# Late modulation dots issued behind the MLP's norms; other planned durations and per-head state tiles in the recurrence

## The chip, the cores and the metric

The program runs on one core of one Trainium2 chip. The metric is the device time of one execution in microseconds; the median of three runs of the kernel before is 4447.88 (4441.65 to 4450.69).

## What is computed

Two blocks follow one another. The first has two layers over a stream `x` of 512 tokens and a context `ctx` of 256, width 1024. Each layer adds a mixer and an MLP to the stream, each between norms whose gains and shifts come from the condition vector (the modulation):

```python
mod = (silu_c @ ada_w[i] + ada_b[i])[:, None, :]
mod_c = silu_cc @ ada_w[i] + ada_b[i]
sh1, sc1, gt1, sh2, sc2, gt2 = jnp.split(mod, N_MOD, axis=-1)
...
x = x + gt1 * rms_norm(y, norm_g[i, 1])
h = modulate(rms_norm(x, norm_g[i, 2]), sh2, sc2)
x = x + gt2 * rms_norm(squared_relu_mlp(h, mlp_w1[i], mlp_w2[i]), norm_g[i, 3])
```

Layer 0's mixer joins pooling and neighbourhood attention; layer 1's is a recurrence over tokens, in both directions, with 16 heads of 64:

```python
S = (S * w_t[:, :, None, :]
     - jnp.einsum('bhij,bhj->bhi', S, kk_t)[..., None] * kka_t[:, :, None, :]
     + v_t[..., None] * k_t[:, :, None, :])
y = jnp.einsum('bhij,bhj->bhi', S, inp[5]) if emit else None
```

The second block (two more layers with gated MLPs, a convolution and two attentions) takes the rest of the time, and the change doesn't touch it.

## The kernel before, in words

**Stages, by the trace's time.** Up to 85 us first sums and the memory; 85 to 440 layer 0's mixer; 440 to 560 its output product (weights `ev_o`) and the norms after it; 560 to 1060 layer 0's MLP over 76 weight blocks (`m0w`); 1060 to 1390 the shift and the products of layer 1's mixer; 1390 to 2050 the recurrence; then layer 1's MLP and the second block.

**Engines.** TensorE (PE) multiplies. Weights arrive in `wr` by a DMA on SyncE's queue (SP), 128 x 1024 in 512 KB; ScalarE (ACT) rounds them to `wh`, and VectorE (DVE), or GpSimd (POOL) for some, subtracts to get the rest `wl`. Tiles `a` hold activations, `t` temporaries, `ps`, `pj`, `ch`, `hq` PSUM results. All recorded calls stand at line 176, those of the planned list at line 171; of the two, a row is told by its tiles.

**Modulation dots.** A modulation column needs 128 x 1024 of `ada_w` (a load `ada`, 512 KB, from a ring of two buffers) and, for each of the two condition vectors (`c_rows`, `cc_rows`), one DVE instruction that multiplies, sums over the 1024 columns and writes `mod` (a dot, with its product thrown to `junk`), followed by a short read of the accumulator. `ada_dot` issues it and `ada_g` goes through the columns. The last 56 columns (8 of layer 0, 48 of layer 1; 112 dots) are issued by the generator `ada` in `second_half`. It waits for the signals of the MLP's norms, then runs woven with `chain`, `work` and others by a clock that costs each operation. That sets an order of issue; a scheduler behind it may place an instruction earlier on its engine where its data allow, and there the 112 dots stand among layer 0's mixer and its output product, ahead of 560 us.

**The recurrence.** `wkv` records all its steps in a `Plan`: 24 cells (three stages of eight pairs of heads), each with `intra` and four `step`s. `Plan.order` then builds the list of PE, ACT, DVE and POOL by simulation: an operation is ready when what it depends on has ended plus `LAT` (.2 us between engines, .06 on the same one), and of those that could start within `SLACK` of the earliest on an engine the one of lowest rank goes first. `SWITCH` is a cost on PE for a change of its tile form. The durations stand in `Step.product` and `Plan.add`. The list is then fixed (`manual_schedule`). Dependencies in the plan are by tile name.

In `step`, a product of `SC` and the state `HV` gives X; ACT copies it to `Xs`; the product `ch<-Xs,TTz` gives U for two heads, on partitions 0 to 63 and 64 to 127 of one PSUM tile; ACT copies one head's half to `HV` and DVE the other's; then the products `hq<-hv,BCt` read both. `HV` is one tile for both heads, in a ring of three:

```python
s.copy(HV[hs[0], at(st), 0], U[hs[0]])
v.tensor_copy(HV[hs[1], at(st), 1], U[hs[1]])
```

Of the kernel before, what the change touches and what calls it, by code (L numbers as in the profile page):

```python
# [2 lines left out]

# [1 line left out]

# [8 lines left out]
ALU = mybir.AluOpType  # L14
# [3 lines left out]
P = 128  # L18
# [8 lines left out]
class Clock:  # L27
# [3 lines left out]
    LAT = 0.2  # L31

    def __init__(self):
        self.free, self.wrote, self.used = {}, {}, {}
        self.now = self.end = 0.0
        self.events = {}
        self.fresh = []
        self.taken = self.given = 0
        self.plan = None

    def op(self, eng, cost, out, ins, lat=LAT):
        at = max(self.free.get(eng, 0.0), self.now)
# [111 lines left out]
class Engine:  # L154
# [5 lines left out]
    def __getattr__(self, fn):  # L160
        real, clock, eng = getattr(self._r, fn), self._c, self._n

        def call(*a, **k):
            aps = [x for x in list(a) + list(k.values()) if isinstance(x, bass.AP)]
            out = k.get("out", a[0] if a else None)
            ins = [x for x in aps if x is not out]
            outs = [out.tensor.name]
            if "accum_out" in k:
                outs.append(k["accum_out"].tensor.name)
            if clock.plan is not None:  # L170
                return clock.plan.add(eng, fn, lambda: real(*a, **k), out, ins, outs)  # L171
            if eng == "DMA":
                clock.dma(outs[0], [x.tensor.name for x in ins], out.shape[0] * _size(out) * 4)
            else:
                clock.op(eng, _cost(eng, fn, out, ins), outs, [x.tensor.name for x in ins])
            return real(*a, **k)  # L176

        setattr(self, fn, call)
        return call


class Step:
# [8 lines left out]
    def product(self, fn, out, ins):  # L191

        k, m, n = ins[0].shape[0], _size(ins[0]), _size(out)
        rows = (0, 1) if k > 64 else (int(ins[0].start_partition() >= 64),)
        cols = (0, 1) if m > 64 else (int(out.start_partition() >= 64),)
        part = [(r, x) for r in rows for x in cols]
        mode = k > 64, m > 64
        if self.mode is None:
            self.first = mode
        elif mode != self.mode:  # L200
            self.at = self.cost + 0.1
        self.mode = mode
        plain = ins[0].dtype == F32
        once = max(0.00084 * n, 0.054) if plain else 0.00042 * n + 0.003
        at = max([self.at] + [self.array.get(p, 0.0) for p in part])
        fin = at + once * (2 if plain and fn != "transpose" else 1)
        for p in part:
            self.array[p] = fin
        self.at = at + 0.006
        self.cost = max(self.cost, fin)  # L210


class Plan:
# [1 line left out]

    LAT = 0.2

    def __init__(self):  # L220
        self.steps, self.rank = [], 0
# [3 lines left out]
    def add(self, eng, fn, call, out, ins, outs):  # L225
        st = self.steps[-1] if self.steps else None
        if not (st and eng == st.eng == "PE" and st.rank[0] == self.rank):
            st = Step(eng, outs[0], (self.rank, len(self.steps)))
            self.steps.append(st)
        i = len(self.steps) - 1  # L230
        st.calls.append(call)
        for x in ins:
            t = x.tensor.name
            if t in self.writer:
                st.deps.add(self.writer[t])
            self.readers.setdefault(t, set()).add(i)
            self.touch.setdefault(t, set()).add(i)
        for t in outs:
            if t in self.writer:
                st.deps.add(self.writer[t])  # L240
            st.deps |= self.readers.get(t, set())
            self.readers[t] = set()
            self.writer[t] = i
            self.touch.setdefault(t, set()).add(i)
        st.deps.discard(i)
        if eng == "PE":
            st.product(fn, out, ins)
        elif eng == "DMA":
            st.cost = 0.1 + out.shape[0] * _size(out) * 4 / 270e3
        else:  # L250
            n = _size(out if fn != "reduce_sum" else ins[0])
            if eng == "ACT":
                st.cost = 0.17 + 0.00082 * n
            elif eng == "DVE":
                st.cost = 0.16 + 0.00105 * n
            elif fn == "tensor_tensor":
                st.cost = 0.2 + 0.0024 * n
            else:
                st.cost = 0.18 + 0.0009 * n

# [5 lines left out]
    def order(self):  # L266
        steps = self.steps
# [18 lines left out]
        mode, out = None, []  # L286
        while any(can.values()):
            best = None
            for eng, c in can.items():
                if not c:  # L290
                    continue
                f = free.get(eng, 0.0)
                at = {}
# [15 lines left out]
                i = min((x for x in at if at[x] <= lo + self.SLACK), key=lambda x: steps[x].rank)  # L309
# [20 lines left out]
                if not rest[x]:  # L330
                    room[self.place[x]].append(last[x])
            for j in s.next:
                lat = self.LAT if steps[j].eng != s.eng else 0.0 if s.eng == "PE" else 0.06
                ready[j] = max(ready[j], fin[i] + lat)
                left[j] -= 1
                if not left[j]:
                    can[steps[j].eng].add(j)
# [1 line left out]
        self.time = max(fin)  # L339
        return [steps[i] for _, i in sorted(out)]  # L340

    SWITCH = 0.1
    SLACK = 0.1


class Queues:
# [312 lines left out]
def tiles_mod(tiles):  # L659
    return [t[0] for t in tiles]  # L660
# [5 lines left out]
class First:  # L666
# [35 lines left out]
            c.nc.sync.dma_start(out[h], c.A["adaT"][i, m][:, h * 512:(h + 1) * 512])  # L702
        return out

    def ada_dot(self, i, mod, m, w, junk):

        for s in range(2):
            o = mod[s][:, m:m + 1]
            for h in range(len(w)):
                n = D // len(w)  # L710
                self.c.nc.vector.tensor_tensor_reduce(
                    out=junk[:, :n], in0=w[h], in1=self.sil[s][:, h * n:(h + 1) * n], scale=1.0,
                    scalar=o if h else self.adab[:, i, m:m + 1], op0=ALU.mult, op1=ALU.add, accum_out=o)
            yield

    def junk(self):
        return self.silp.tile([P, D], mybir.dt.bfloat16, name=self.c.nm("junk"), tag="junk")

    def ada_g(self, i, mod, ms):
        c, nc = self.c, self.c.nc  # L720
        for m in ms:
            w = c.ring(self.silp, [P, D], "ada", 2)
            nc.sync.dma_start(w, c.A["adaT"][i, m])
            yield from self.ada_dot(i, mod, m, [w], self.junk())

    def ada_tiles(self):
        c = self.c
# [468 lines left out]
    def second_half(self, yh, mtiles, mod, dr):  # L1196
# [47 lines left out]
        def ada():  # L1244

            for i in range(2):
                yield ("h", i, KD - 1)
            yield from self.ada_g(0, tiles_mod(mtiles), range(40, 48))
            self.ada_gains(0, mtiles, (3,))
            yield from self.ada1()  # L1250
            self.sil_es.close()
            odd.open()
            sig("ada1")
# [94 lines left out]
        nc.sync.dma_start(dr["mk"][l], kv)  # L1348
        yield

    def ada1(self):
        tiles = self.ada_tiles()
        self.mod1 = self.ada_out(tiles)
        yield from self.ada_g(1, tiles_mod(tiles), range(48))
        self.ada_gains(1, tiles, range(4))


# [48 lines left out]
    def cell(self, i, b, p, dr, ytm, bonus):  # L1406
# [99 lines left out]
            yield ("chain", i - 3)  # L1506


        HV = self.wt([8, 2, 64], "hv", 3)
        for h in range(2):  # L1510
            rr = np.s_[64 - h * 64:128 - h * 64]
            for d in range(2):
                nc.sync.dma_start(HV[rr, d * 4:(d + 1) * 4, h], dr["v"][tok[d], p * P + h * 64:p * P + (h + 1) * 64].rearrange("(c s) f -> s c f", s=64))
        for h in range(2):
            rr = np.s_[h * 64:(h + 1) * 64]
            g.tensor_copy(HV[rr, 0:8:7, h], self.H[p][rr])
        SC, BCt, TT = yield from self.intra(i, out, BC, AQ)
        done("intra")
        for st in range(4):
# [115 lines left out]
    def step(self, p, qd, st, SC, BCt, TT, Qz, HV, wc, ytm):  # L1635
# [10 lines left out]
        half = lambda: c.bank("ch", (P, 2, 64))  # L1646
        X = half()
        for d, h in DH:
            mm(X[hs[h], d], SC[d][:, h, chs[d], :64], HV[:, es[d], h], start=d == 0, stop=d == 1)
        Xs = self.wt([2, 64], "Xs", 3)  # L1650
        s.copy(Xs, X)
        HQ = c.bank("hq", (P, 2, 2, 64))
        HU, Q = HQ[:, 0], HQ[:, 1]
        for d, h in DH:
            mm(HU[hs[h], d], c.ident[:, hs[h]], HV[:, es[d], h], start=d == 0, stop=False)
        if out:

            for h, d in DH:
                mm(Q[hs[d], h], Qz[:, es[d], h], HV[:, es[d], h], start=False, stop=False)
        yield  # L1660
        U = half()
        for d, h in DH:
            mm(U[hs[h], d], TT[:, es[d], h], Xs[:, d], start=d == 0, stop=d == 1)
        s.copy(HV[hs[0], at(st), 0], U[hs[0]])
        v.tensor_copy(HV[hs[1], at(st), 1], U[hs[1]])
        yield
        for d, h in DH:
            mm(HU[hs[h], d], BCt[:, es[d], h], HV[:, es[d], h], start=False, stop=d == 1 and not out)
        if out:
            for h, d in DH:  # L1670
                mm(Q[hs[d], h], SC[d][:, h, chs[d], 64:128], HV[:, es[d], h], start=False, stop=h == 1)
        if st < 3:
            for h in range(2):
                v.tensor_tensor(HV[hs[h], at(st + 1), h], HU[hs[h]], wc[hs[h], at(st)].unsqueeze(2).to_broadcast([64, 2, 64]), op=ALU.mult)
        else:
            v.tensor_tensor(self.H[p], HU, wc[:, at(st)].unsqueeze(2).to_broadcast([P, 2, 64]), op=ALU.mult)
        if out:
# [1128 lines left out]
```

## Time and profile before

| | us |
|---|---|
| median of three runs | 4447.88 |
| lowest and highest | 4441.65, 4450.69 |
| profiled execution | 4443.47 |
| its span | 4441.7 |
| PE busy | 4102.2 (92%) |
| DVE busy | 2478.7 (56%) |
| ACT busy | 1754.9 (40%) |
| POOL busy | 1097.0 (25%) |
| TensorE clock granted, mean | .954 |

Shares are of the span. An engine's idle time counts only where PE, or something that PE waits for, waits on it; so the stretches that the change touches are read one by one. A wait for several semaphores is put down to the one that came last.

### The profile page before, as it was taken

Reading aid. Unit: us, or ns where it says so; the run is one execution under the profiler, and the core shown is the slowest. Engines: PE = TensorE matmul, PEld = TensorE weight load, DVE = VectorE, ACT = ScalarE, POOL = GpSimd, SP = SyncE. Lnnn points to the kernel's source line nnn. Section 1 sums busy time; section 2 is a strip of 40 time slices with the busy share of each in tenths; the row PEclk is TensorE's granted clock in tenths of the full one; section 3 lists DMA queues with packets and bytes.
Section 4 is the critical chain, followed back from the end, with each engine's and each line's share of the span. In section 5 each row is a group of like instructions: output and inputs, shape, how many; then the busy total and the mean of one; then the engine's idle time right before and its main releaser. Section 6 shows DMA issues by size and latency. Waiting matters only on the chain. (4 is left out here: it accounts for less than half of the span.)

```text
span 4441.7 us, 76269 instructions
## 1 busy us (share of the span) xinstructions
PE 4102.2 (92%) x31520; PEld 3414.6 (77%) x31520; DVE 2478.7 (56%) x3961; ACT 1754.9 (40%) x3289; POOL 1097.0 (25%) x1095
## 2 busy tenths in 40 slices
PE   5897899999798999988999999979999999989998
PEld 4786688887586777777888788866888888767887
DVE  8999844445852555675744533486333433684333
ACT  4455422223443766654523422325222422344222
POOL 4223300002523334453100211254110300353001
PEclk8888999999898989998999999989999999989999
DMA  6444522123233111113433233320333333212332
GB/s 220 149 133 124 171 72 62 62 67 100 75 119 115 42 51 46 51 36 101 131 99 96 91 100 96 102 64 29 95 100 90 100 95 100 91 34 71 96 96 85
DMA packets 187339, 406.08 MB, mean 91 GB/s; under 512 B 46016, under 2 KB 80880, under 8 KB 186992
## 3 DMA queue, kind: packets, MB, share of 16 engines
q1 hardware_dynamic: 186992, 401.22, 29.3%
q8 instruction: 247, 4.05, 0.4%
q14 instruction: 100, 0.82, 0.1%
HBM read 383.32 MB, written 17.83 MB: 90 GB/s over the span
## 5 line engine op out<-in xcount | busy, mean ns | idle before, releaser
L176 PE MATMUL pj<-a,wh 128*128 128x512 f32 (+1 forms) x5328 | 1417.6, 355 | 74.8 <-DVE a L176 37.2
L176 PE MATMUL ps<-a,wh 128*128 128x512 f32 x4192 | 1293.7, 390 | 12.2 <-DVE a L176 6.6
L176 ACT CAST wh<-wr 128x1024 fp32r<-128x1024 f32 (+3 forms) x548 | 565.2, 1032 | 1643.1 <-PE ps L176 951.5
L176 PEld LDWEIGHTS pj<-a,wh 128*128 128x128 f32 x5328 | 949.5, 194 | 223.5 <-issue 42.6
L176 PE MATMUL pj<-a,wl 128*128 128x512 f32 (+1 forms) x2664 | 938.3, 353 | 25.9 <-DVE wl L176 21.6
L176 PEld LDWEIGHTS ps<-a,wh 128*128 128x128 f32 x4192 | 786.6, 188 | 177.4 <-DVE a L176 7.6
L176 PE MATMUL ps<-a,wl 128*128 128x512 f32 x2096 | 815.5, 389 | 0.0
L176 DVE TENSOR_TENSOR wl<-wr,wh 128x1024 fp32r<-128x1024 f32 (+3 forms) x490 | 597.3, 1219 | 301.6 <-ACT wh L176 268.4
L176 PEld LDWEIGHTS pj<-a,wl 128*128 128x128 f32 x2664 | 516.4, 194 | 101.7 <-DVE wl L176 27.9
L176 PEld LDWEIGHTS ps<-a,wl 128*128 128x128 f32 x2096 | 393.9, 188 | 81.3
L176 POOL TENSOR_TENSOR t<-t,a 128x512 f32<-128x512 f32 x94 | 159.6, 1700 | 1113.3 <-ACT t L176 1113.3
L176 POOL TENSOR_TENSOR a<-a,t 128x512 f32<-128x512 f32 (+1 forms) x109 | 142.5, 1310 | 1020.6 <-ACT t L176 1019.2
L176 PE MATMUL ps<-a,a 128*128 128x256 f32 (+4 forms) x859 | 190.4, 371 | 37.0 <-ACT a L176 15.7
L176 DVE SCALAR_TENSOR_TENSOR ytm<-ps,ytm 128x512 f32<-128x512 f32 x96 | 66.4, 692 | 265.6 <-PE ps L176 265.6
L176 DVE TENSOR_TENSOR t<-t,ps 128x512 f32<-128x512 f32 x87 | 59.8, 688 | 274.5 <-PE ps L176 270.0
L171 ACT CAST f<-ps 128x512 f16<-128x512 f32 x312 | 177.4, 587 | 79.0 <-PE ps L171 73.3
L176 DVE TENSOR_TENSOR a<-a,pj 128x512 f32<-128x512 f32 (+1 forms) x176 | 101.1, 578 | 167.2 <-PE pj L176 167.2
L176 PEld LDWEIGHTS ps<-a,a 128*128 128x128 f32 (+1 forms) x859 | 133.2, 206 | 73.2 <-ACT a L176 25.4
L176 POOL TENSOR_TENSOR wl<-wr,wh 128x1024 fp32r<-128x1024 f32 x58 | 149.1, 2576 | 143.8 <-ACT wh L176 124.9
L176 DVE TENSOR_TENSOR t<-ps,a 128x512 f32<-128x512 f32 x86 | 59.2, 691 | 220.6 <-PE ps L176 220.6
L176 DVE SCALAR_TENSOR_TENSOR a<-a,c_cvw,a 128x511 f32<-128x511 f32 (+15 forms) x180 | 177.5, 1006 | 2.3
L176 ACT CAST a<-t 128x512 fp32r<-128x512 f32 (+1 forms) x206 | 116.3, 565 | 115.5 <-DVE t L176 115.2
(321 smaller groups left out, 5359.2 us busy)
## 6 DMA issues: line engine op xcount, KB each, us to landing
wr<-in_f1w SPq DMA_DIRECT2D x120, 512.0 KB
wr<-in_f2w SPq DMA_DIRECT2D x120, 512.0 KB
ada<-in_adaT SPq DMA_DIRECT2D x88, 512.0 KB
wr<-in_m0w SPq DMA_DIRECT2D x76, 512.0 KB
wr<-in_m1w SPq DMA_DIRECT2D x76, 512.0 KB
wr<-in_ev_o SPq DMA_DIRECT2D x16, 512.0 KB
wr<-in_w_o SPq DMA_DIRECT2D x16, 512.0 KB
k<-d_k SPq DMA_DIRECT2D x48, 128.0 KB
```

Of the source, the lines that this page charges most:

```text
L171: return clock.plan.add(eng, fn, lambda: real(*a, **k), out, ins, outs)
L176: return real(*a, **k)
```

## The change

**A.** `Engine.call` keeps the last instruction of each engine in `clock.last`. When `ada` starts (both MLP norms signalled), it takes the last DVE instruction, and each of the 112 dots is issued under `issue_after` that instruction: the scheduler may no longer place it ahead.

**B.** In the plan: PE's durations a little longer, `scalar_tensor_tensor` on DVE .2 us longer, POOL's `tensor_tensor` 1.65 us where it has 8 columns or fewer, a hop of .2 us from PE, .1 from a DMA and .07 from other engines (.03 on the same one), `SWITCH` .11, `SLACK` .2.

**C.** The state tile `HV` becomes two tiles, one by head, in a ring of six.

```diff
+            clock.last[eng] = r = real(*a, **k)
+            return r
...
-        once = max(0.00084 * n, 0.054) if plain else 0.00042 * n + 0.003
+        once = max(0.0009 * n, 0.06) if plain else 0.00045 * n + 0.005
...
-    LAT = 0.2
+    LAT = {"PE": 0.2, "DMA": 0.1}
...
-                st.cost = 0.16 + 0.00105 * n
+                st.cost = 0.16 + 0.00105 * n + (0.2 if fn == "scalar_tensor_tensor" else 0.0)
             elif fn == "tensor_tensor":
-                st.cost = 0.2 + 0.0024 * n
+                st.cost = 0.2 + 0.0022 * n if n > 8 else 1.65
...
-                lat = self.LAT if steps[j].eng != s.eng else 0.0 if s.eng == "PE" else 0.06
+                lat = self.LAT.get(s.eng, 0.07) if steps[j].eng != s.eng else 0.0 if s.eng == "PE" else 0.03
...
-    SWITCH = 0.1
-    SLACK = 0.1
+    SWITCH = 0.11
+    SLACK = 0.2
...
+                with self.c.tc.issue_after(after) if after else nullcontext():
+                    self.c.nc.vector.tensor_tensor_reduce(
+                        out=junk[:, :n], in0=w[h], in1=self.sil[s][:, h * n:(h + 1) * n], scale=1.0,
+                        scalar=o if h else self.adab[:, i, m:m + 1], op0=ALU.mult, op1=ALU.add, accum_out=o)
...
-            yield from self.ada_g(0, tiles_mod(mtiles), range(40, 48))
+            after = c.clock.last["DVE"].ins
+            yield from self.ada_g(0, tiles_mod(mtiles), range(40, 48), after)
             self.ada_gains(0, mtiles, (3,))
-            yield from self.ada1()
+            yield from self.ada1(after)
...
-        HV = self.wt([8, 2, 64], "hv", 3)
+        HV = [self.wt([8, 64], "hv", 6) for _ in range(2)]
...
-        s.copy(HV[hs[0], at(st), 0], U[hs[0]])
-        v.tensor_copy(HV[hs[1], at(st), 1], U[hs[1]])
+        s.copy(HV[0][hs[0], at(st)], U[hs[0]])
+        v.tensor_copy(HV[1][hs[1], at(st)], U[hs[1]])
```

Every engine has as many instructions as before; the order differs in two places only, from 200 to 850 us and in the recurrence. On DVE, between two weight splits of the MLP (one weight block), before:

```order
L176 TENSOR_TENSOR wl_5944<-wr_5941,wh_5943 128x1024
L176 TENSOR_TENSOR a_4022<-a_4022,pj_5947 128x512
L176 TENSOR_TENSOR a_4027<-a_4027,pj_5948 128x256
L176 TENSOR_TENSOR a_4023<-a_4023,pj_5980 128x512
L176 TENSOR_TENSOR a_4027<-a_4027,pj_5981 128x256
L176 TENSOR_TENSOR wl_6016<-wr_6013,wh_6015 128x1024
```

And on the same engine and block with the change (an `ISA` row with `junk` is a dot, the one after it the accumulator's read):

```order
L177 TENSOR_TENSOR wl_5944<-wr_5941,wh_5943 128x1024
L177 ISA junk_6182,mod_5402<-ada_6180,cc_rows_108,c_adab 128x1024
L177 ISA mod_5402 128x1
L177 TENSOR_TENSOR a_4022<-a_4022,pj_5947 128x512
L177 TENSOR_TENSOR a_4027<-a_4027,pj_5948 128x256
L177 ISA junk_6257,mod_5400<-ada_6255,c_rows_105,c_adab 128x1024
...
L177 ISA junk_6257,mod_5402<-ada_6255,cc_rows_108,c_adab 128x1024
...
L177 TENSOR_TENSOR a_4023<-a_4023,pj_5980 128x512
L177 ISA junk_6330,mod_5400<-ada_6328,c_rows_105,c_adab 128x1024
...
L177 TENSOR_TENSOR a_4027<-a_4027,pj_5981 128x256
L177 TENSOR_TENSOR wl_6016<-wr_6013,wh_6015 128x1024
```

Four dots and their reads now stand between the two splits.

On SP, the loads of the same stretch with the change (before, the `wr` rows followed one another and all `ada` loads had been issued earlier):

```order
L177 DMA wr_5797<-in_m0w 128x2x512
L177 DMA ada_5916<-in_adaT 128x1024
L177 DMA ada_5955<-in_adaT 128x1024
L177 DMA wr_5869<-in_m0w 128x2x512
L177 DMA ada_5988<-in_adaT 128x1024
L177 DMA ada_6027<-in_adaT 128x1024
L177 DMA wr_5941<-in_m0w 128x1024
```

Each weight load has two loads for the dots behind it, where it had none.

On PE, one step of the recurrence (the same cell and step), before: from the product U to the products that need both its copies.

```order
L171 MATMUL ch_12892<-Xs_12890,TTz_11835 64x64 x4
L171 LDWEIGHTS MB_12990
L171 MATMUL ps_13002<-c_iq,MB_12990 64x64
...
L171 MATMUL ps_12949<-f_3467_12946,c_i_11793 64x512
...
L171 MATMUL ps_12949<-f_3469_12948,GT_12916 64x64
...
L171 MATMUL ps_13003<-c_iq,c_i_11793 64x512
...
L171 MATMUL ps_13003<-c_iq,GT_12992 64x64
...
L171 MATMUL hq_12891<-hv_12837,BCt_12841 64x64 x4
```

And with the change:

```order
L172 MATMUL ch_12906<-Xs_12904,TTz_11835 64x64 x4
L172 LDWEIGHTS f_3477_12956
L172 MATMUL ps_12957<-c_i_11793,f_3477_12956 64x64
...
L172 MATMUL hq_12905<-hv_12850,BCt_12855 64x64
L172 MATMUL hq_12905<-hv_12851,BCt_12855 64x64
```

Between the two products stand 52 matmuls of other cells before and 16 with the change.

The copies of that U, with what they wait for: DVE before (its wait is ACT's copy of the other head),

```order
L171 TENSOR_TENSOR ML_12991<-SC_12997,MB_12990 64x256 [waits Activation_49]
L171 TENSOR_TENSOR GT_12992<-ps_13002,c_lvl 128x512 [waits PE_49]
L171 COPY hv_12837<-ch_12892 64x2x64 [waits Activation_49]
L171 TENSOR_SCALAR sw_13311<-sw_13311 128x512
L171 TENSOR_TENSOR hv_12837<-hq_12891,wc_12832 64x2x64 [waits PE_49]
L171 TENSOR_TENSOR hv_12837<-hq_12891,wc_12832 64x2x64 [waits Activation_49]
```

and with the change, where ACT writes `hv_12850` and DVE `hv_12851`:

```order
L172 TENSOR_TENSOR ML_13007<-SC_13010,MB_13006 64x256 [waits Activation_49]
L172 TENSOR_TENSOR hv_12850<-hq_12901,wc_12845 64x2x64 [waits PE_49]
L172 TENSOR_TENSOR hv_12851<-hq_12901,wc_12845 64x2x64 [waits Activation_49]
L172 COPY hv_12851<-ch_12906 64x2x64 [waits DVE_49,Activation_49]
L172 TENSOR_TENSOR SC_13013<-ps_13015,c_scmask 128x512
L172 TENSOR_TENSOR hv_12850<-hq_12905,wc_12845 64x128 [waits PE_49,Activation_49]
```

The copy still waits on ACT; it stands earlier among DVE's other work.

## Rows read from the trace of the kernel before

**Rows 1.** Busy time by stretch: before 440, output product, recurrence (columns first).

```profile
core 0: us, PE busy (x) PEld busy (x) DVE busy (x) ACT busy (x) POOL busy (x), PEclk, DMA share, GB/s
213.00:440.00 227.00, 183.99 (x1069) 158.35 (x1068) 208.46 (x446) 125.61 (x302) 67.92 (x52) 0.87 0.41 125
440.00:560.00 120.00, 106.51 (x530) 84.36 (x530) 97.86 (x132) 51.12 (x86) 42.21 (x30) 0.94 0.54 170
...
1430.00:2040.00 610.00, 556.55 (x13855) 468.07 (x13851) 375.89 (x772) 394.83 (x913) 258.15 (x400) 0.93 0.16 44
```

**Rows 2.** Busy time in the MLP, columns as in rows 1.

```profile
600.00:1000.00 400.00, 400.00 (x2294) 352.92 (x2293) 162.37 (x239) 96.06 (x144) 0.00 (x0) 1.00 0.21 64
```

**Rows 3.** The dots alone, as in rows 1: DVE busy, PEclk, DMA share, GB/s.

```profile
213.00:440.00 227.00, 121.48 (x81) 0.87 0.41 125
440.00:560.00 120.00, 45.55 (x31) 0.94 0.54 170
```

**Rows 4.** Timeline of DVE: start, duration, instruction (a read, then a dot).

```profile
272.60 0.08 DVE L176 DVE_READ_ACCUMULATOR2_ANT mod<- 128x1 f32 x1
272.71 1.28 DVE L176 CUSTOM_DVE_ANT_0 junk<-ada,cc_rows,c_adab 128x1024 bf16<-128x1024 f32 x1
```

**Rows 5.** PE's waits, 213 to 440: awaited, us in total, times, longest.

```profile
PE ps L176 <- DVE a L176: 12.9, 6, 4.5
PE ps L176 <- ACT a L176: 12.2, 8, 3.1
PE pj L176 <- DVE a L176: 7.3, 4, 5.1
...
PE pj L176 <- POOL wl L176: 2.8, 2, 1.7
```

**Rows 6.** PE's waits, 440 to 560.

```profile
PE pj L176 <- DVE wl L176: 4.3, 3, 3.2
```

**Rows 7.** Timeline at the mixer's end (in brackets idle time before, and releaser).

```profile
433.26 1.74 DVE L176 CUSTOM_DVE_ANT_0 junk<-ada,c_rows,c_adab 128x1024 bf16<-128x1024 f32 x1
...
434.93 1.20 DVE L176 TENSOR_TENSOR a<-a,a 128x512 fp32r<-128x512 f32 x1
...
436.19 0.80 PE L176 MATMUL pj<-a,wh 128*128 128x512 f32 x1 [5.13 <-DVE a L176]
```

**Rows 8.** DVE's groups, 600 to 1000: count, busy us, mean ns, idle before.

```profile
L176 DVE TENSOR_TENSOR wl<-wr,wh 128x1024 fp32r<-128x1024 f32 x48 | 58.8, 1225 | 40.7 <-ACT wh L176 40.7
```

**Rows 9.** PE's waits in the recurrence, 1430 to 2040.

```profile
PE ps L171 <- ACT f L171: 11.6, 28, 1.3
PE ps L171 <- DVE th L171: 11.1, 12, 2.9
PE ps L171 <- DVE GT L171: 8.7, 9, 2.1
PE hq L171 <- DVE hv L171: 5.1, 7, 1.5
...
PE hq L171 <- ACT hv L171: 1.7, 4, 0.9
```

**Rows 10.** Waits of all engines, 1430 to 2040: DVE's copy of U for ACT's.

```profile
DVE hv L171 <- ACT hv L171: 57.4, 51, 3.4
```

**Rows 11.** Timeline of one step of the recurrence.

```profile
1501.23 0.40 PE L171 MATMUL ch<-Xs,TTz 128*64 128x64 f32 x8
...
1501.56 0.44 PE L171 MATMUL ps<-f,MB 64*64 64x64 f16 x16
...
1501.68 0.26 ACT L171 COPY hv<-ch 64x128 f32<-64x128 f32 x1 [1.16 <-PE ch L171]
...
1502.76 0.29 DVE L171 COPY hv<-ch 64x128 f32<-64x128 f32 x1
```

**Rows 12.** DVE's groups, 1430 to 2040.

```profile
L171 DVE SCALAR_TENSOR_TENSOR BC<-th,iW 64x512 f32<-64x512 f32 x43 | 39.5, 919 | 5.4 <-PE ps L171 4.9
```

**Rows 13.** The dots between 458 and 489, columns as in rows 3.

```profile
458.00:489.00 31.00, 24.12 (x16) 0.98 0.65 204
```

More of the change, by code (lines that the diff above doesn't have):

```diff
@@ L1 @@
 import heapq
-from contextlib import ExitStack, contextmanager
+from contextlib import ExitStack, contextmanager, nullcontext
 import numpy as np
@@ L39, in __init__ @@
         self.plan = None
+        self.last = {}
     def op(self, eng, cost, out, ins, lat=LAT):
@@ L175, in call @@
                 clock.op(eng, _cost(eng, fn, out, ins), outs, [x.tensor.name for x in ins])
-            return real(*a, **k)
+            clock.last[eng] = r = real(*a, **k)
+            return r
         setattr(self, fn, call)
@@ L703, in ada_load, with ada_dot @@
         return out
-    def ada_dot(self, i, mod, m, w, junk):
+    def ada_dot(self, i, mod, m, w, junk, after=None):
         for s in range(2):
@@ L710, in ada_dot @@
                 n = D // len(w)
-                self.c.nc.vector.tensor_tensor_reduce(
-                    out=junk[:, :n], in0=w[h], in1=self.sil[s][:, h * n:(h + 1) * n], scale=1.0,
-                    scalar=o if h else self.adab[:, i, m:m + 1], op0=ALU.mult, op1=ALU.add, accum_out=o)
+                with self.c.tc.issue_after(after) if after else nullcontext():
+                    self.c.nc.vector.tensor_tensor_reduce(
+                        out=junk[:, :n], in0=w[h], in1=self.sil[s][:, h * n:(h + 1) * n], scale=1.0,
+                        scalar=o if h else self.adab[:, i, m:m + 1], op0=ALU.mult, op1=ALU.add, accum_out=o)
             yield
@@ L717, in junk, with ada_g @@
         return self.silp.tile([P, D], mybir.dt.bfloat16, name=self.c.nm("junk"), tag="junk")
-    def ada_g(self, i, mod, ms):
+    def ada_g(self, i, mod, ms, after=None):
         c, nc = self.c, self.c.nc
@@ L723, in ada_g @@
             nc.sync.dma_start(w, c.A["adaT"][i, m])
-            yield from self.ada_dot(i, mod, m, [w], self.junk())
+            yield from self.ada_dot(i, mod, m, [w], self.junk(), after)
     def ada_tiles(self):
@@ L1349, in memory_end, with ada1 @@
         yield
-    def ada1(self):
+    def ada1(self, after):
         tiles = self.ada_tiles()
         self.mod1 = self.ada_out(tiles)
-        yield from self.ada_g(1, tiles_mod(tiles), range(48))
+        yield from self.ada_g(1, tiles_mod(tiles), range(48), after)
         self.ada_gains(1, tiles, range(4))
@@ L1512, in cell @@
             for d in range(2):
-                nc.sync.dma_start(HV[rr, d * 4:(d + 1) * 4, h], dr["v"][tok[d], p * P + h * 64:p * P + (h + 1) * 64].rearrange("(c s) f -> s c f", s=64))
+                nc.sync.dma_start(HV[h][rr, d * 4:(d + 1) * 4], dr["v"][tok[d], p * P + h * 64:p * P + (h + 1) * 64].rearrange("(c s) f -> s c f", s=64))
         for h in range(2):
             rr = np.s_[h * 64:(h + 1) * 64]
-            g.tensor_copy(HV[rr, 0:8:7, h], self.H[p][rr])
+            g.tensor_copy(HV[h][rr, 0:8:7], self.H[p][rr])
         SC, BCt, TT = yield from self.intra(i, out, BC, AQ)
@@ L1648, in step @@
         for d, h in DH:
-            mm(X[hs[h], d], SC[d][:, h, chs[d], :64], HV[:, es[d], h], start=d == 0, stop=d == 1)
+            mm(X[hs[h], d], SC[d][:, h, chs[d], :64], HV[h][:, es[d]], start=d == 0, stop=d == 1)
         Xs = self.wt([2, 64], "Xs", 3)
@@ L1654, in step @@
         for d, h in DH:
-            mm(HU[hs[h], d], c.ident[:, hs[h]], HV[:, es[d], h], start=d == 0, stop=False)
+            mm(HU[hs[h], d], c.ident[:, hs[h]], HV[h][:, es[d]], start=d == 0, stop=False)
         if out:
             for h, d in DH:
-                mm(Q[hs[d], h], Qz[:, es[d], h], HV[:, es[d], h], start=False, stop=False)
+                mm(Q[hs[d], h], Qz[:, es[d], h], HV[h][:, es[d]], start=False, stop=False)
         yield
@@ L1663, in step @@
             mm(U[hs[h], d], TT[:, es[d], h], Xs[:, d], start=d == 0, stop=d == 1)
-        s.copy(HV[hs[0], at(st), 0], U[hs[0]])
-        v.tensor_copy(HV[hs[1], at(st), 1], U[hs[1]])
+        s.copy(HV[0][hs[0], at(st)], U[hs[0]])
+        v.tensor_copy(HV[1][hs[1], at(st)], U[hs[1]])
         yield
         for d, h in DH:
-            mm(HU[hs[h], d], BCt[:, es[d], h], HV[:, es[d], h], start=False, stop=d == 1 and not out)
+            mm(HU[hs[h], d], BCt[:, es[d], h], HV[h][:, es[d]], start=False, stop=d == 1 and not out)
         if out:
             for h, d in DH:
-                mm(Q[hs[d], h], SC[d][:, h, chs[d], 64:128], HV[:, es[d], h], start=False, stop=h == 1)
+                mm(Q[hs[d], h], SC[d][:, h, chs[d], 64:128], HV[h][:, es[d]], start=False, stop=h == 1)
         if st < 3:
             for h in range(2):
-                v.tensor_tensor(HV[hs[h], at(st + 1), h], HU[hs[h]], wc[hs[h], at(st)].unsqueeze(2).to_broadcast([64, 2, 64]), op=ALU.mult)
+                v.tensor_tensor(HV[h][hs[h], at(st + 1)], HU[hs[h]], wc[hs[h], at(st)].unsqueeze(2).to_broadcast([64, 2, 64]), op=ALU.mult)
         else:
```

## The prediction, made before the changed kernel ran

> **What bounds the kernel now.** I read the busy time by stretch first [rows 1]: TensorE (PE) is the busiest engine in each, but it covers only 183.99 of 227 us between 213 and 440, 106.51 of 120 up to 560 and 556.55 of 610 in the recurrence; in the layer-0 MLP it works without a gap, 400 of 400 us [rows 2]. So PE sets the end, and what an edit is worth is PE's idle time and half clock in the stretches that it touches. [...] Next I asked for the share of the modulation dots in DVE's work [rows 3]: 121.48 of its 208.46 us in the first stretch, 45.55 of 97.86 in the second; one of them in the timeline [rows 4] shows what it costs, 1.28 us and .08 to read the accumulator (the mean of the 81 is 1.50). Then PE's waits [rows 5, 6] and the tail of the mixer in the timeline [rows 7]; for the MLP the busy time per weight block [rows 2, 8]; for the recurrence PE's waits and those of all engines [rows 9, 10], one step of the chain in the timeline [rows 11] and DVE's durations [rows 12].
>
> The profiled execution took 4443.47, a span of 4441.70 and 1.77 around it; the median shown is 4.4 above it. I sum from 4446, between the two.
>
> **Part A, the dots.** 112 dots (81 and 31, [rows 3]) leave the stretches before 560 and run in the MLP.
>
> What they free. Both stretches have 43.0 + 13.5 = 56.5 us of PE idle [rows 1]. Of that 12.9 + 7.3 + 2.8 + 4.3 = 27.3 is put down to DVE or to a split on POOL [rows 5, 6], the engines on which dots stand in the way; 12.2 to ACT, which has work of its own there. The tail shows the mechanism [rows 7]: the split `a<-a,a` that PE has awaited for 5.13 us starts at 434.93 because a dot ran from 433.26. I take three quarters of the 27.3 (a chain of splits stays behind each dot) = 20.5, a quarter of the 12.2 = 3. The clock falls short by .13 x 227 + .06 x 120 = 36.7 us, some 30 while PE works (81% and 89% busy); the stretches with idle are the ones under 1.00, and with under half of the idle gone I take 12. Together **-36**. Bounds: -10 if only the 5.1 and 4.5 us that are the longest of their rows go; -76 if all of 27.3 + 12.2 + 36.7 does. What is late next there is ACT's own 12.2.
>
> What they cost. In the MLP 48 weight blocks take 400 us of PE without a gap, 8.33 each, and DVE 162.37 / 48 = 3.38 each [rows 2, 8]; POOL is idle there, so I take the undisturbed dot, 1.28 + .08 = 1.36 [rows 4], not the mean of 1.50. The new list puts four dots between two splits `wl` over some 25 blocks: 3.38 + 4 x 1.36 = 8.82 against 8.33. DVE becomes the slower one by .49, 25 x .49 = **+12**. DVE's free time, which would hide the dots, is thus used up: the MLP's additions and splits queue behind them on DVE, and PE waits for `wl`. Bounds: 0, if the blocks loaded ahead absorb it; +34 if a dot costs 1.50 as in the mean of [rows 3] (121.48 / 81): 3.38 + 4 x 1.58 = 9.70, 1.37 x 25. The loads: SP now issues two dot loads after each weight load, and each waits for one of two buffers. Between 458 and 489 eight such loads (16 dots) came in 31 us at 204 GB/s [rows 13], 3.9 each; the MLP leaves 8.82 / 2 = 4.4 each, so I cost them at nothing, covered by those .5 us. Without that cover the weights, queued behind on SP, are late and PE waits for them.
>
> **Parts B and C, the recurrence.** Same instructions, another order. B corrects durations: a `scalar_tensor_tensor` of 512 columns was planned at .70 us and takes .92 [rows 12]; now .90. A hop from ACT or DVE to another engine was .2 and is .07; the trace has .05 (product `ch<-Xs,TTz` ends at 1501.63, ACT's copy starts at 1501.68, [rows 11]). The wait for `th`, 11.1 us [rows 9], comes from the under-planned instruction; I let 8 go. Waits for ACT `f` and DVE `GT`, 11.6 + 8.7, are one-hop waits on evictions; a third goes with truer hops, -6.
>
> C gives each head its own state tile, so the planner may put ACT's and DVE's copies of U side by side. In the program they are not free: DVE's copy waits on ACT's in all 96 steps before, in 71 after, and in the other 25 ACT's waits on DVE's; what orders them is the PSUM tile that both read. So **C does not do what it plans**: the 57.4 us of DVE `hv<-ACT hv` [rows 10] stays. But the list now believes it. Between the product U and `hq<-hv,BCt`, which needs both copies, it leaves less other PE work: counted over the 96 steps, 16 matmuls or fewer in 12 before and 49 after, 17 or 18 in 7 and 22, 32 or more in 50 and 19. The chain there is .05 hop, .26 ACT, .05, .29 DVE, .05 = .70 us; sixteen small matmuls end at 1502.00, .37 after U [rows 11]. PE's waits there were 5.1 + 1.7 = 6.8 us [rows 9] over the 19 short steps, .36 each; 71 short steps give 25, so +18. Clock: the stage lost .07 x 610 = 42.7 us beside 53.4 idle, .8 per idle us, so (18 - 8) x .8 = +8. Sum 18 - 8 - 6 + 8 = **+12**. Bounds: -25 if U's waits stay as they are, (8 + 6) x 1.8; +41 as in the first rival.
>
> [...]
>
> Sum: 4446 - 36 + 12 + 12 = **4434**, with 4412 to 4452 as this case's own range.
>
> **Rivals.**
> 1. Slower: the serial copies stall every short step. Besides .70 - .37 = .33, DVE is 375.89 / 610 = 62% busy [rows 1], and its copy queues: in [rows 11] it starts .82 after ACT's has ended, where a hop is .05. With a quarter of that on average, .2: 71 x .53 - 6.8 = +31; less 8 for `th`; clock .8 x 23 = +18: +41. With a poor stretch A (-24, as DVE's chain of splits stays) that is 4446 - 24 + 41 = 4463. It decides once the recurrence gives back over 33. For it: the 57.4 us and the counts. Against it: the old list's 19 short steps cost PE only .36 each.
> 2. The dots sat in DVE's free time and delayed nothing: first stretches -10, MLP +12, recurrence +12: 4460. For it: most of a DVE wait of PE is the split itself. Against it: 92% busy DVE in 213 to 440 and [rows 7].
> 3. Faster: U is no bound, because the copies run at once: .05 + .29 + .05 = .39 after U, against .37 of the shortest filler; then the truer durations keep their -14, x 1.8 with the clock -25, and with A's -24 that is 4397. For it: `th` and the hops were plainly wrong by the rows. Against it: the waits that stay in the program; so most of its chance is a filler that is long enough after all.
>
> **How the numbers follow.** My sum .45; rival 3 .23; rival 2 .15; rival 1 .17. The range, 4388 to 4470, takes in all four centres with the bounds of A on the near side. A measurement of this kernel can tell .2%, 8.9 us, from no change: below 4439 is faster, above 4457 slower. My sum splits .32, .11, .02; the third rival .23 all faster; the second 0, .05, .10; the first 0, .04, .13: faster .55, same .20, slower .25.
>
> **What would show it.** Right: no dot before 560 and DVE there under 100 us in 213 to 440; PE's waits on DVE `a` under 8 and the clock over .90; in the MLP a row PE `<-DVE wl` of about 10 us, DVE busy over 90% for 25 blocks; in the recurrence `hq<-DVE hv` up from 5.1 to 20 or more, `th` down to 3. Wrong: MLP blocks still 8.33 us apart, or weights late by DMA; `hq` waits unchanged though the fillers are short, which would mean that the copies come earlier than the chain says; waits on `a` before 560 unchanged with the dots gone. The step that I trust least is the share of the 27.3 us that goes, and with it the clock's 12.

## The result and the profile after

The changed kernel takes 4400.85 us (median, 4399.56 to 4401.75) against 4445.02 of the kernel before in the same comparison: a ratio of .9899, interval .9882 to .9916, so 44 us (1.0%) faster. The forecast was 4434; 4400.85 lies outside the case's own range of 4412 to 4452 and inside the wider one, 4388 to 4470.

The profiled executions differ by 41.7 us (4441.7 and 4400.0). Where that came from is read from landmarks, the issue times of loads that stand at the same place of both programs:

| landmark (us from the start) | before | after | difference | in this stage |
|---|---|---|---|---|
| last load of `x` before the output product | 441.6 | 405.8 | -35.8 | -35.8 |
| first weights of the MLP | 524.6 | 486.4 | -38.1 | -2.3 |
| last weights of the MLP | 1095.7 | 1070.8 | -24.9 | +13.2 |
| first load of the recurrence | 1389.2 | 1365.5 | -23.7 | +1.2 |
| first load behind it | 2056.6 | 2013.2 | -43.4 | -19.7 |
| end of the span | 4441.7 | 4400.0 | -41.7 | +1.7 |

So the mixer gave 38, the MLP took 13, and the recurrence gave 20, where 36, 12 and a loss of 12 were forecast.

Busy time of the changed kernel by stretch, the first two as in [rows 1], then the same work as in [rows 1]'s first two by the landmarks (they end 35.8 and 38.1 us earlier), then 120 us of the MLP with dots, then the recurrence between its landmarks; columns as there.

```profile
213.00:440.00 227.00, 202.25 (x1205) 175.36 (x1205) 98.59 (x285) 136.26 (x319) 61.64 (x56) 0.94 0.19 59
440.00:560.00 120.00, 108.47 (x590) 87.82 (x589) 75.73 (x115) 54.92 (x99) 38.59 (x30) 0.94 0.35 106
213.00:404.20 191.20, 166.48 (x1057) 145.94 (x1056) 89.01 (x277) 123.51 (x301) 52.49 (x49) 0.94 0.13 39
404.20:521.90 117.70, 109.56 (x540) 87.18 (x541) 51.71 (x67) 52.26 (x89) 43.75 (x34) 0.94 0.36 110
600.00:720.00 120.00, 114.08 (x638) 99.40 (x637) 110.88 (x184) 24.37 (x37) 0.00 (x0) 0.97 0.59 180
1365.50:2013.20 647.70, 578.82 (x14166) 486.15 (x14167) 411.04 (x820) 418.91 (x957) 272.07 (x438) 0.94 0.20 54
```

For the same work, PE's idle time fell from 56.5 to 32.9 us (24.7 and 8.1) and its busy time from 290.5 to 276.0. The dots alone, as in [rows 3].

```profile
213.00:440.00 227.00, 0.00 (x0) 0.94 0.19 59
440.00:560.00 120.00, 13.47 (x11) 0.94 0.35 106
```

The second stretch now holds the MLP's start, hence 11 dots. In the MLP the dots and splits of the changed kernel's DVE, 486 to 785 (count, busy us, mean ns, idle before):

```profile
L177 DVE CUSTOM_DVE_ANT_0 junk<-ada,cc_rows,c_adab 128x1024 bf16<-128x1024 f32 x56 | 72.0, 1287 | 0.5
L177 DVE CUSTOM_DVE_ANT_0 junk<-ada,c_rows,c_adab 128x1024 bf16<-128x1024 f32 x56 | 71.8, 1283 | 16.4 <-DMA ada<-in_adaT 15.7
L177 DVE TENSOR_TENSOR wl<-wr,wh 128x1024 fp32r<-128x1024 f32 x38 | 47.0, 1237 | 7.5 <-ACT wh L177 7.2
```

All 112 are here at 1.28 us, with little POOL work beside them (17.25 of 299 us); in the trace before, from 213 to 560, the 64 dots with no POOL instruction beside them took 1.26 to 1.29 us, the 48 with one 1.77 on average. DVE is 92% busy from 600 to 720 (110.88 of 120) and PE has lost 5.9 of 120 us, where it had no idle in [rows 2]. DVE itself stood 15.7 us for the dots' own loads `ada`. PE's waits over the work of [rows 5] (213 to 404.2):

```profile
PE ps L177 <- DVE a L177: 6.6, 4, 2.6
PE ps L177 <- ACT a L177: 6.4, 7, 1.8
PE pj L177 <- ACT a L177: 4.5, 1, 4.5
PE pj L177 <- DVE a L177: 2.7, 1, 2.7
PE pj L177 <- POOL wl L177: 2.4, 2, 1.3
```

DVE `a` falls from 20.2 to 9.3 and the wait of `ps` for ACT `a` from 12.2 to 6.4. In the MLP (486 to 1050):

```profile
PE pj L177 <- DVE a L177: 5.4, 5, 2.1
PE pj L177 <- ACT a L177: 4.9, 5, 1.8
PE pj L177 <- ACT wh L177: 3.7, 4, 2.4
PE ps L177 <- POOL a L177: 3.4, 2, 2.1
PE pj L177 <- DVE wl L177: 0.9, 2, 0.8
```

PE waits for the hidden tiles `a`, whose square and split queue on DVE behind the dots (in its timeline a square of .69 us at 660.31 and a split of .69 at 663.55 each follow a dot's read of .08), and hardly for `wl`. In the recurrence (1365.5 to 2013.2), against [rows 9]:

```profile
PE ps L172 <- ACT f L172: 9.1, 22, 0.9
...
PE hq L172 <- DVE hv L172: 5.8, 6, 2.3
PE ps L172 <- DVE GT L172: 4.7, 9, 0.9
PE hq L172 <- ACT hv L172: 4.5, 14, 0.5
PE ps L172 <- DVE th L172: 4.5, 1, 4.5
```

`th` is down by 6.6, `GT` by 4.0, `f` by 2.5, and the `hq` waits are up by 3.5 only (20 of them, where [rows 9] had 11; the whole stage before had 13, of 7.5 us). That is one of the prediction's signs of being wrong: the `hq` waits hardly changed though the fillers are short. The order of the copies stays, as forecast (all engines' waits; [rows 10] had 57.4 in a slightly shorter window):

```profile
DVE hv L172 <- ACT hv L172: 56.1, 58, 4.6
...
ACT hv L172 <- DVE hv L172: 6.6, 21, 0.9
```

And the timeline of one short step, against [rows 11]:

```profile
1629.59 0.40 PE L172 MATMUL ch<-Xs,TTz 128*64 128x64 f32 x8
...
1629.93 0.44 PE L172 MATMUL ps<-c_i,f 64*64 64x64 f16 x16
1630.05 0.26 ACT L172 COPY hv<-ch 64x128 f32<-64x128 f32 x1 [0.56 <-PE ch L172]
1630.34 0.29 DVE L172 COPY hv<-ch 64x128 f32<-64x128 f32 x1 [0.46 <-ACT hv L172]
...
1630.36 0.72 PE L172 MATMUL hq<-hv,BCt 128*64 128x64 f32 x7
```

The first `hq` product starts at 1630.36, .05 after ACT's copy ends at 1630.31 and while DVE's still runs to 1630.63. It didn't need both copies. This .05 is a hop from ACT; the prediction's .05 in [rows 11] is one from PE. PE then stands inside the group: the seven take .72 us, where eight of the same products take .45 in the kernel before, behind a long filler:

```profile
1503.17 0.45 PE L171 MATMUL hq<-hv,BCt 128*64 128x64 f32 x8
```

So the trace counts the second wait, at least in this step, as PE's busy time.

### The profile page after: what moved, and what is told of

Its sections match the earlier page's. It is cut to its first block, busy times and chain, and to the rows that moved or that the text cites. A ratio compares the mean times of both kernels' runs of the same rounds, so it can differ in the third digit from the quotient of the medians.

```text
span 4400.0 us, 76274 instructions
## 1 busy us (share of the span) xinstructions
PE 4085.2 (93%) x31520; PEld 3401.2 (77%) x31520; DVE 2458.0 (56%) x3961; ACT 1754.1 (40%) x3289; POOL 1078.8 (25%) x1095
```

## The experiments

Each is timed against the kernel before on the same chip; groups of experiments ran on different chips, so between groups the ratios are to be compared. "Stage" is the recurrence between its two landmarks, in the profiled execution; its idle is the length less PE's busy time.

### The parts alone

Part A alone is the diff of A put on the kernel before. 

> Part A alone (late dots), recurrence as before. Theory 'separate parts': the landmarks of the traces say that A gives 36 us before the MLP and costs 13 in it, so 4422 with the recurrence unchanged. Rival 'A shifts the clock of what follows': the recurrence's list is the same, but its half-clock time falls too, and the run is near 4410.

Measured: 4422.37 against 4445.74, ratio .9946 (.9931 to .9961). The stage is 667.9, before 667.4. A gives its 23 us and doesn't touch what follows. In its trace the MLP's weights span 588.0 us, 16.8 more than before.

Part B alone (all of B's constants, one state tile). 

> Part B alone (durations, hops, SWITCH, SLACK), one state tile. Theory 'durations': B carries the whole gain of the recurrence, so 4425 (-20), or less, 4418, if C's short fillers cost 7. Rival 'tiles': the gain comes from C, and B alone is within 6 us of before.

Measured: 4409.24 against 4445.74, .9915 (.9900 to .9930), -36. That is more than the whole change gave in the recurrence.

Part C alone. 

> Part C alone (state tiles by head), old durations. Theory 'durations': C only shortens the fillers behind U, so the run is 0 to 10 us slower than before (4445 to 4455). Rival 'tiles': the shorter steps let the chain of states run ahead and C alone gives 10 to 20 us.

Measured: 4440.86 against 4445.74, .9988 (.9978 to .9997): some 5 us faster (1 to 10 by the interval), neither theory's number.

B with C, no A. 

> B and C without A. Theory 'separate parts': the recurrence's 20 us and nothing else, 4425. If A and the recurrence help one another, 4435.

Measured: 4430.83 against 4445.74, .9962 (.9948 to .9977), -15, between the two numbers. So C, put on B, costs 21.6 us. The stage before, with B, and with B and C (busy time, columns as in [rows 1], one kernel after the other):

```profile
1389.20:2056.60 667.40, 587.66 (x14166) 494.42 (x14167) 402.60 (x820) 416.47 (x957) 274.21 (x431) 0.91 0.19 53
```

```profile
1390.00:2018.50 628.50, 566.95 (x14167) 479.35 (x14168) 399.06 (x820) 418.31 (x957) 275.43 (x431) 0.95 0.20 56
```

```profile
1396.10:2045.60 649.50, 580.30 (x14167) 487.82 (x14168) 411.41 (x820) 418.53 (x957) 271.18 (x431) 0.94 0.20 54
```

Idle 79.7, 61.6 and 69.2. B took 18 us of idle and lifted the clock from .91 to .95. C gave 7.6 of idle back, and 13.4 of PE's busy time. The `hq<-hv,BCt` products are part of that; PE's group with B alone, then with B and C:

```profile
L171 PE MATMUL hq<-hv,BCt 128*64 128x64 f32 x768 | 51.1, 237 | 4.2 <-DVE hv L171 3.0 <-ACT hv L171 1.0
```

```profile
L171 PE MATMUL hq<-hv,BCt 128*64 128x64 f32 x768 | 58.5, 240 | 12.0 <-DVE hv L171 6.7 <-ACT hv L171 4.4
```

7.8 us more idle ahead of and between them, and 7.4 more busy.

### Is it the tiles, or what the list believes of them?

```diff
         v.tensor_copy(HV[1][hs[1], at(st)], U[hs[1]])
+        steps = c.clock.plan.steps
+        steps[-1].deps.add(len(steps) - 2)
```

B and C, with the plan told that DVE's copy follows ACT's. 

> B and C, but the plan is told that DVE's copy of U follows ACT's (one dependency more in the list's simulation, the program's instructions are the same). Theory 'belief', that the list leaves too little work behind U because it takes the copies for parallel: back to B alone, 4409 (within 8), fillers behind U as in B alone. Rival 'tiles', that the two tiles themselves cost: 4431 as B with C.

Measured: 4405.95 against 4446.95, .9908 (.9894 to .9923). The 21.6 us are back, with the two tiles in place. In the traces, 71 of the 96 steps have 18 matmuls or fewer behind U with B and C, 29 with B alone, 27 here; with C alone, under the old durations, they are 34, which fits that C alone cost nothing. The stage:

```profile
1390.80:2015.90 625.10, 567.02 (x14166) 479.42 (x14167) 401.90 (x820) 417.68 (x957) 270.98 (x431) 0.95 0.21 56
```

So the two tiles cost nothing of themselves; the loss is the list's belief that the copies run side by side. By which waits it is lost is shown only in part. The group that needs the copies, with the told plan:

```profile
L171 PE MATMUL hq<-hv,BCt 128*64 128x64 f32 x768 | 53.7, 239 | 10.8 <-DVE hv L171 9.1 <-ACT hv L171 1.6
```

Against B and C that is 1.2 us less idle and 4.8 less busy, 6 of the 24 by which the stage is shorter; the rest lies in other waits and in PE's busy time elsewhere.

### A and B without C

> A and B, one state tile as before. Parts add: -23 (A alone) and -36 (B alone) from 4446 give 4387, 14 us under the changed kernel's 4401, and the wait inside the products on hv and BCt as in B alone. Rival, that A and C only pay together (A alone and B with C added give 4408, the whole change 4401): near 4400.

Measured: 4386.81 against 4446.95, .9861 (.9844 to .9877). A and B add (.9946 x .9915 = .9861), and without C the change is 14 us better by the medians, 17 by the ratios (.9899 and .9861, whose intervals don't meet). A alone and B with C multiply to .9908, inside the whole change's interval, so no help of A and C for one another is shown.

### Which of B's numbers

Hops alone (`LAT`, and .03 on one engine). 

> Of B only the hops between engines (.2 to .07, .1 behind a DMA, .06 to .03 on one engine). Theory 'hops', that the old list ordered the work around waits that do not exist: more than half of B's 36, 4420 or less, with the waits on f and GT falling and th's 11 us still there. Rival 'durations': within 8 us of before.

Measured: 4437.91 against 4446.95, .9979 (.9969 to .9988). `scalar_tensor_tensor` alone. 

> Of B only the .2 us more for a scalar_tensor_tensor on DVE. Theory 'durations', with th's wait of 11.1 us as the sign: th falls to 3 and with the clock's share the run gives 15 to 20 us, 4428. Rival 'hops': th's wait falls, but another takes its place, within 6 us of before.

Measured: 4441.48 against 4446.95, .9987 (.9978 to .9997). Both together. 

> Of B the hops and the stt's .2 together, without PE's and POOL's durations, SWITCH and SLACK. Alone they gave 9 and 5 us with the stage's idle at 80. Theory 'together', that a list is only as good as its worst number: near B without SLACK, a ratio of .993 (-31) and idle near 66. Theory 'sum': -14, a ratio of .997. Rival 'PE's and POOL's durations carry it': not past -14.

Measured: 4436.04 against 4445.85, .9974 (.9962 to .9986), -12: the two only add. `SWITCH` and `SLACK` alone. 

> Of B only SLACK .2 and SWITCH .11, old durations and hops. Theory 'slack', that B's 20 us of idle time come from a wider choice by rank (the older cell first), since hops and the stt alone left the stage's 80 us of idle as they were: 4420 or less, idle of the stage near 65. Rival 'together', that only durations, hops and slack together do it: 4436 to 4446, idle near 80.

Measured: 4436.47 against 4450.07, .9972 (.9961 to .9983), -13. B without these two. 

> B without SLACK and SWITCH: all durations and hops new, the choice as narrow as before. Theory 'slack': little is left, 4430 to 4440, idle of the stage near 78. Rival 'together': 4409 to 4420.

Measured: 4416.43 against 4450.07, .9930 (.9913 to .9946), -31. The stage with hops and stt, then with all of B but `SWITCH` and `SLACK`:

```profile
1392.00:2045.70 653.70, 578.34 (x14167) 484.69 (x14167) 394.36 (x820) 417.70 (x957) 269.55 (x432) 0.94 0.19 54
```

```profile
1399.30:2027.50 628.20, 561.94 (x14167) 473.47 (x14168) 395.11 (x820) 414.35 (x957) 269.00 (x431) 0.96 0.20 56
```

Idle 75.4 and 66.3. Between the two runs stand PE's and POOL's durations, some 20 us of effect (.9974 to .9930). The slack theory fell: alone it gives 13 with an idle of 78.3, and on top of the rest some 7, with intervals that overlap (.9930 and .9915). That the hops or th's duration carry B fell too: in each of the two runs alone `th` dropped from 11.1 to 4.3 or 2.7 while other waits rose and the idle stayed at 79 to 81. `th` fell to 4.2 and 4.0 also with `SLACK` and `SWITCH` alone and with C alone, which leave the planned `scalar_tensor_tensor` as it was; so the 11.1 us are not shown to come from that duration. Whether PE's or POOL's numbers are the stronger, and whether either alone would do, was not tried. Nor were neighbouring values: each run is one list of a simulation, and how much of a small gain is the luck of one list is open. In the trace POOL's small `tensor_tensor` (`gv`, 128 x 8) takes 1.70 us where the old list had .22.

### The dots paced

One column for each weight block, each behind the last DVE instruction at that point, on A and B with one state tile (`tick` signals a block's start):

```diff
-            yield from self.ada_g(0, tiles_mod(mtiles), range(40, 48), after)
+            for m in range(40, 48):
+                yield ("block", m - 40 + 6)
+                yield from self.ada_g(0, tiles_mod(mtiles), [m], c.clock.last["DVE"].ins)
...
+        for m in range(48):
+            yield ("block", m + 8 + 6)
+            yield from self.ada_g(1, tiles_mod(tiles), [m], self.c.clock.last["DVE"].ins)
```

> A and B with one state tile, and the late dots paced: one column (two dots) for each weight block of the MLP, behind the last DVE instruction at that point, in place of four dots for each of 28 blocks. Theory 'DVE is the slower one there': 3.38 + 2 x 1.37 = 6.1 us of DVE for 8.33 of PE, so the 13 us that the MLP lost come back, 4374, and the 284 us of the changed kernel's dots are spread over 450. Rival, that the loads in SP's queue cost them: the same loads still stand there, 4380 to 4387.

Measured: 4373.46 against 4450.07, .9833 (.9818 to .9847), the fastest of all. The MLP's weights span 572.7 us (571.2 before, 584.4 in the changed kernel, 590.0 with A and B). Busy time of its MLP, columns as in [rows 1]:

```profile
600.00:720.00 120.00, 120.00 (x695) 105.89 (x694) 80.81 (x128) 27.31 (x40) 0.00 (x0) 1.00 0.40 124
600.00:1000.00 400.00, 400.00 (x2273) 351.47 (x2272) 272.48 (x434) 96.42 (x143) 0.00 (x0) 1.00 0.41 123
```

and PE's waits in it, 486 to 1040:

```profile
PE pj L178 <- ACT wh L178: 4.6, 5, 2.2
...
PE pj L178 <- ACT a L178: 0.9, 1, 0.9
PE pj L178 <- DVE a L178: 0.2, 1, 0.2
```

PE is without a gap again, DVE 67% busy in the first row, and the 10 us of waits on `a` are 1.1. This doesn't part the dots from their loads: as many loads stand in SP's queue, but one for each weight block where there were two. The changed kernel's waits for loads from 520 to 785:

```profile
DVE junk L177 <- DMA ada<-in_adaT: 15.7, 16, 1.8
...
ACT wh L177 <- DMA wr<-in_m0w: 1.5, 1, 1.5
```

The weights were not late (1.6 us before, 560 to 860). But DVE stood for the dots' loads, with all that comes behind a dot on it, and that can be part of the 13.

## Why the prediction was right or wrong

**Part A, what it frees: right** in size and mechanism. -36 was forecast, 23.5 of idle and 12 by the clock; -38 was measured to the MLP's first weights, 23.6 of idle and 14.5 of busy time, while the clock went from .87 to .94. Of the 173 windows of 2 us from 213 to 559 in the trace before, the granted clock is 1.00 in 130, .50 in 26 and between them in 17: the half clock that the prediction speaks of. Within the idle the shares were wrong and made up for one another: the rows of DVE and of splits fell by about half (27.3 to 12.8, of which 1.1 lies behind 404.2) where I let three quarters go, so DVE `a` stayed above the 8 that I named; ACT `a` fell by half (12.2 to 6.4) and not by a quarter, and some 3 us went from rows of POOL and ACT that I hadn't counted.

**Part A, what it costs: right** in size, +12 against +13.2 (16.8 in A alone, 18.9 with A and B), with DVE 92% busy there. The named wait was wrong: not `wl` (.9) but the hidden tiles `a` (5.4 from DVE, which stand behind the same queue, and 4.9 from ACT, which I read as late for DVE in turn). The loads, which I costed at nothing, held DVE up for 15.7 us; the paced run took two dots and one load from each block together, so it doesn't say how the 13 divide.

**Recurrence, B: mis-sized,** some -20 with its clock against -36. The step was "I let 8 go" for `th`, "a third goes with truer hops, -6", and with it the rule that only the net of idle moves the clock. I read single waits and took each wrong number of the list for the price of the wait beside it. B alone gave 36: its stage has 18 us less idle and 21 less busy time for the same matmuls, with the clock at .95 for .91. Hops, `scalar_tensor_tensor` and `SLACK` with `SWITCH` by themselves only moved waits about and left the idle as it was; it fell to 75 with the first two together and to 66 when PE's and POOL's durations came in. Those I hadn't costed at all, and they bring about half of the 36.

**Recurrence, C: right in sign, too dear.** The claim that C doesn't do what it plans, and that its belief costs, is shown by the told plan. I had +18 and its clock, .8 x 18 = 14, so 32; C on B costs 21.6. Two things were wrong in the working: "which needs both copies" (the first product needs ACT's alone, so the chain ahead of it is .36 and not .70), and .36 a short step: the short steps went from 19 to 71 and the `hq` waits only from 11 to 20, 3.5 us more. More of the loss shows as busy time of the same products (51.1 to 58.5 us) and in other waits. And it is no cost of C by itself: with the old durations C is some 5 us faster than before.

**The sum.** The recurrence came out at -20 where +12 was forecast: that is nearly the whole miss of 33 us, and that the wide range held the time is owed to the third rival. This rival, 4397, lay nearest the time by luck: its mechanism, copies that run at once, is not what happened (they wait as before), and its -25 met a gain of 36 less a cost of 21.6. In the traces before and with the change the two copies of a step don't overlap in any of the 96 pairs. That the PSUM tile which both read orders them is my reading of the program: with the change the copies write a tile each and share only `ch`, and the wait is still there. Whether they would run at once with U in two tiles of their own wasn't tried.

## What to carry to other kernels

A planner's wrong number is not priced by the wait that stands beside it: `th`'s wait fell by 8.4 us with its duration put right, and the run gained 5. Three corrections gave 5 to 13 us each alone, and about half of B came from durations that none of the waits I had read pointed at. Whether the parts do more together than they add up to is not shown, as PE's and POOL's durations didn't run alone. A change that makes the planner freer than the program (two tiles where an order remains) loses what the planner then leaves out; give the plan the order that the program has. Work moved under a busier engine's cover is to be paced to that cover: two dots and one load for each block were nearly free (1.5 us), four and two cost 13 to 19.

## What the runs showed that I had not expected

A wait in the midst of a group of matmuls appeared as PE's busy time in the short step shown above (.72 us for seven products, where eight took .45), and with C put on B `hq<-hv,BCt` rose from 51.1 to 58.5 us for the same 768 products while its idle rose from 4.2 to 12.0. And PE's busy time for the same matmuls moved as much as its idle: with B alone 20.7 us beside 18.2, as the granted clock of the stage went from .91 to .95. It moved without the idle too: with the hops, the `scalar_tensor_tensor`, `SLACK` with `SWITCH` or C alone the stage's idle stayed at 78 to 81 us, its busy time was 8 to 13 us shorter and the clock .93 or .94, while with A alone, whose list for the recurrence is the old one, it stayed at 588.2 (587.7 before). These are single profiled executions; they speak against my .8 us of clock for each us of idle.
